# Relu and row sum: the first load of 128 descriptors goes as two loads of 64

## The chip, the cores and the metric

The kernel runs on one core of a Trainium2 chip. The metric is the device time of one execution in microseconds (us), the median of a few runs. Three engines matter here: ScalarE (ACT in the profile) and VectorE (DVE) compute, and SyncE (SP) issues the loads and stores. The data itself is moved by 16 DMA engines that the core shares among all transfers; a profile counts a transfer's time from its issue on SP to its landing, when the last of its pieces has counted up the transfer's semaphore.

## The reference

```python
batch, seq, dim = 32, 512, 1024
x = np.random.randn(batch, seq, dim).astype(np.float32)

def reference(x):
    relu_x = np.maximum(x, 0)
    return np.sum(relu_x, axis=-1).astype(np.float32)
```

So 16,384 rows of 1,024 float32 numbers (67.1 MB) are read, negative numbers become zero, each row is summed, and 16,384 sums (65.5 KB) are written.

## The kernel before

**Regions.** The 16,384 rows are cut along `REGIONS = [1, 111, 16]` (L8) into three parts. In each part every one of the 128 partitions of the on-chip memory holds a stretch of neighbouring rows: 1 row each in the first part, 111 in the second, 16 in the third. Every partition has 128 rows in all. Only the first part is one row deep, so its 128 rows lie next to each other in the input.

**Chunks.** The rows go through three buffers (`buf[:, c % NB, ...]`, L51) of 16 rows per partition, 8 MB each. `CHUNKS` (L9) lists seven full chunks. Chunk 0 is the only one made of two loads: one row of each partition out of the first region, then 15 rows of each out of the second. Each of the six others is one load of 16 rows of each partition. After them come tail loads of 8, 4 and 2 rows, and the last two rows of each partition are cut into four pieces of 912, 512, 256 and 368 numbers (L108 to L115).

**Order of the loads.** All loads are issued by SP in the order in which the loop at L85 writes them, on one queue. From chunk 3 on, each waits until DVE has finished the chunk that used the same buffer (L87). A load over 128 partitions is made of 128 descriptors, one contiguous stretch each: 4 KB in the first load, 60 KB in the second, 64 KB in the chunks after it. The two loads of chunk 0 are moved by hand to the very start of SP's program:

```python
if c == 0:
    code.insert(arrival, code.pop())
    arrival += 1
```

`arrival` is the place ahead of SP's first drain, which belongs to the barrier that all engines pass at the start. So the first two loads are issued before the barrier and everything else behind it.

**Compute.** Both loads of chunk 0 count up the same semaphore `s_in[0]`, by 16 each, and ACT waits for their sum (L140) before it applies relu to the whole chunk in one instruction (L145, 16,384 numbers per partition). DVE then reduces rows in groups (L160). In the later chunks ACT works in pieces, and the last chunk and the tail are split row by row between the two engines, each with an instruction that does relu and sum together (`on_act`, L127; `on_dve`, L130). When the last pieces have landed and been summed, SP stores the sums (L117, L123, L207) and waits for the stores.

Of the kernel before, what the change touches and what calls it, by code (L numbers as in the profile page):

```python
# [3 lines left out]
P = 128  # L4
D = 1024
BIG = 16
NB = 3
REGIONS = [1, 111, 16]  # L8
CHUNKS = [[(0, 0, 1), (1, 0, 15)]] + [[(1, 16 * c + 15, 16)] for c in range(6)]  # L9
ACT_STEPS = [[16], [7, 9], [7, 9], [7, 9], [4, 5, 7], [3, 4, 5]]  # L10
DVE_STEPS = [[4, 5, 7], [7, 4, 5], [7, 4, 5], [7, 4, 5], [4, 5, 7], [3, 4, 5]]
TAIL = [8, 4, 2]
# [4 lines left out]
def bass_relu_sum_kernel(  # L17
# [20 lines left out]
    J = B * S // P  # L38
    NBIG = len(CHUNKS)
    assert BIG * NBIG + sum(TAIL) + 2 == J == sum(REGIONS)  # L40
# [4 lines left out]
    xv = [  # L45
        xr[P * s : P * (s + n), :].rearrange("(p j) d -> p j d", p=P)
        for s, n in zip(start, REGIONS)
    ]
    ov = [of[P * s : P * (s + n)].rearrange("(p j) -> p j", p=P) for s, n in zip(start, REGIONS)]

    buf = nc.alloc_sbuf_tensor("buf", [P, NB, BIG, D], fp32)  # L51
# [6 lines left out]
    s_in = [nc.alloc_semaphore(f"s_in{i}") for i in range(n_in)]  # L58
# [11 lines left out]
    sp, act, dve = nc.sync, nc.scalar, nc.vector  # L70

    NTWO = len(ACT_STEPS)
    done = [sum(map(len, DVE_STEPS[: c + 1])) for c in range(NTWO)]
# [5 lines left out]
    code = nc.main_func.blocks[0].instructions  # L79
    arrival = next(  # L80
        i
        for i, ins in enumerate(code)
        if ins.engine == mybir.EngineType.SP and type(ins).__name__ == "InstDrain"
    )
    for c in range(NBIG + 1):  # L85
        if c >= NB:
            sp.wait_ge(s_dve, done[c - NB])  # L87
        if c < NBIG:
            i = 0
            for g, j, n in CHUNKS[c]:  # L90
                sp.dma_start(  # L91
                    out=buf[:, c % NB, i : i + n, :], in_=xv[g][:, j : j + n, :]
                ).then_inc(s_in[c], 16)
                i += n
                if c == 0:
                    code.insert(arrival, code.pop())
                    arrival += 1
    r = 0
    tail = []
    for i, n in enumerate(TAIL):  # L100
# [10 lines left out]
    for k, (lo, hi) in enumerate((first, second, third)):  # L111
# [6 lines left out]
        out=of[0:P].rearrange("(k q) -> k q", q=32), in_=turned[0:P:32, 0:32]  # L118
# [7 lines left out]
    def on_act(t, acc):  # L126
        return act.activation(t, t, AF.Relu, accum_out=acc)  # L127

    def on_dve(t, acc):
        return dve.tensor_scalar(  # L130
            out=t, in0=t, scalar1=0.0, scalar2=None, op0=ALU.max, op1=ALU.add, accum_out=acc
        )

    def row(c, i):
        return buf[:, c % NB, i, :], res[:, c * BIG + i : c * BIG + i + 1]

    k = 0
    for c in range(NTWO):
        alone = BIG - sum(ACT_STEPS[c])
        act.wait_ge(s_in[c], 16 * len(CHUNKS[c]))  # L140
        r = 0
        ready = []
        for n in ACT_STEPS[c]:
            t = buf[:, c % NB, r : r + n, :]
            act.activation(t, t, AF.Relu).then_inc(s_act, 1)  # L145
            k += 1
            ready += [k] * n
            r += n
        for i in range(BIG - alone // 2, BIG):
            on_act(*row(c, i))  # L150
        if alone:
            dve.wait_ge(s_in[c], 16 * len(CHUNKS[c]))
            for i in range(BIG - alone, BIG - alone // 2):
                on_dve(*row(c, i))
        r = seen = 0
        for n in DVE_STEPS[c]:
            if ready[r + n - 1] > seen:
                seen = ready[r + n - 1]
                dve.wait_ge(s_act, seen)
            dve.tensor_reduce(  # L160
                out=res[:, c * BIG + r : c * BIG + r + n],
                in_=buf[:, c % NB, r : r + n, :],
                axis=X,
                op=ALU.add,
            ).then_inc(s_dve, 1)
            r += n
        if c == 1:
            dve.wait_ge(s_dve, done[c])
            dve.transpose(out=turned[:, :], in_=res[:, 0:32]).then_inc(s_turn, 1)  # L169
# [3 lines left out]
    for c in range(NTWO, NBIG):  # L173
        act.wait_ge(s_in[c], 16 * len(CHUNKS[c]))
        dve.wait_ge(s_in[c], 16 * len(CHUNKS[c]))
        for i in range(BIG):
# [10 lines left out]
    lo, hi = first  # L187
# [5 lines left out]
    lo, hi = second  # L193
    act.wait_ge(s_in[-2], 16)
    on_act(flat[:, lo:hi], seam[:, k + HEAD : k + HEAD + 1]).then_inc(s_seam, 1)
    lo, hi = third
# [41 lines left out]
```

## Time and profile before

| | |
|---|---|
| median of 3 runs | 160.88 us (160.72 to 160.93) |
| span of the profiled execution | 159.4 us |
| DVE busy | 120.6 us (76%) |
| ACT busy | 101.5 us (64%) |
| read from memory | 67.11 MB, 421 GB/s over the span |
| the first load, 512 KB | issued at 0.00 us, landed 3.3 us later |
| the second load, 7,680 KB | issued at 0.45 us, landed 21.1 us later |
| last store | issued at 157.93 us, landed 1.4 us later |

The span runs from the first instruction of the program to the last. The first instruction is the issue of the first load. The profiled execution has no time of its own beside its span, so its time is put together: the span of 159.4 us, and about 1.5 us around it that make up the difference to the median of the runs.

Times in the profile are microseconds from the start of the span. A line such as `SPq L91` is SP issuing a load at line 91. `DMA buf<-in_x_dram` is a load into `buf`. In the list of DMA issues the last number is the time from the issue to the landing, and it includes the time in which a load stands in the queue behind earlier ones.

### The profile page before, as it was taken

What the parts mean: (1) busy time and instruction counts of PE and PEld (TensorE: products, weight loads), DVE (VectorE), ACT (ScalarE), POOL (GpSimd) and SP (SyncE); (2) the same over time, 40 slices, a digit from 0 to 9 for tenths busy, and PEclk for the clock granted to TensorE, in tenths of its full rate; (3) what the DMA queues carried; (4) which work ended last, traced back from release to release, by engine and by line L of the source; (5) the groups of instructions that cost most, each with busy time, mean ns of one, the idle gap of its engine ahead of it and who ended that gap; (6) DMA issues with size and microseconds to landing.
All of it is one profiled execution on the core that took longest, in us unless ns stands there. A gap on an engine that the chain in (4) does not pass through costs nothing.

```text
span 159.4 us, 150 instructions
## 1 busy us (share of the span) xinstructions
DVE 120.6 (76%) x59; ACT 101.5 (64%) x54; POOL 0.2 (0%) x4
## 2 busy tenths in 40 slices
DVE  0000000009999999999999999999999999898995
ACT  3000059980799708996099941999329980496975
POOL 0000000000000000000000000000000000000000
DMA  9997996996996997989979969969969979798994
GB/s 378 493 401 339 493 526 263 526 526 263 526 493 296 526 444 345 526 378 411 526 312 477 526 263 526 526 263 526 526 263 526 444 345 526 321 469 374 417 400 142
DMA packets 2457, 67.18 MB, mean 421 GB/s; under 512 B 536, under 2 KB 792, under 8 KB 1176
## 3 DMA queue, kind: packets, MB, share of 16 engines
q1 hardware_dynamic: 2456, 67.18, 98.1%
q14 instruction: 1, 0.01, 0.0%
HBM read 67.11 MB, written 0.07 MB: 421 GB/s over the span
## 4 chain that ended last, share of the span: by engine, by line
DVE 55%; DMA 34%; ACT 9%; SPq 2%; issue 0%
DVE res L160 54%; DMA buf<-in_x_dram 34%; ACT buf L145 9%; SPq L101 1%; SPq L112 1%; DVE buf L130 0%; DVE seam L130 0%; SPq L91 0%; DVE turned L169 0%
## 5 line engine op out<-in xcount | busy, mean ns | idle before, releaser
L160 DVE TENSOR_REDUCE res<-buf 128x4 f32<-128x4096 f32 (+3 forms) x18 | 99.4, 5596 | 35.5 <-ACT buf L145 35.5
L145 ACT ACTIVATE buf<-buf 128x7168 f32<-128x7168 f32 (+5 forms) x13 | 80.4, 6233 | 46.1 <-DMA buf<-in_x_dram 46.1
L127 ACT ACTIVATE buf<-buf 128x1024 f32<-128x1024 f32 (+2 forms) x19 | 19.0, 999 | 8.9 <-DMA buf<-in_x_dram 8.9
L130 DVE TENSOR_SCALAR_CACHE_REDUCE buf<-buf 128x1024 f32<-128x1024 f32 (+2 forms) x19 | 20.7, 1143 | 1.7 <-DMA buf<-in_x_dram 1.6
L127 ACT ACTIVATION_READ_ACCUMULATOR buf<-buf 128x1 f32 x19 | 3.6, 188 | 0.0
L145 ACT ACT_TABLE_LOAD x1 | 1.3, 1283 | 1.3 <-PEq L223 1.3
L130 DVE DVE_READ_ACCUMULATOR buf<-buf 128x1 f32 x19 | 1.6, 84 | 0.0
L130 DVE TENSOR_SCALAR_CACHE_REDUCE seam<-seam 128x258 f32<-128x258 f32 x1 | 0.4, 421 | 0.0
L127 ACT ACTIVATE seam<-seam 128x114 f32<-128x114 f32 x1 | 0.3, 300 | 0.1
L169 DVE STREAM_TRANSPOSE turned<-res 128x32 f32<-128x32 f32 x1 | 0.2, 211 | 0.0
L127 ACT ACTIVATION_READ_ACCUMULATOR seam<-seam 128x1 f32 x1 | 0.2, 186 | 0.0
L223 POOL MEMSET const-bfloat16-1.0<- 128x1 bf16 x1 | 0.1, 101 | 0.0
L223 POOL MEMSET const-uint8-127<- 128x1 uint8 x1 | 0.1, 101 | 0.0
L223 POOL MEMSET const-float32-0.0<- 128x1 f32 x1 | 0.1, 98 | 0.2 <-issue 0.2
L223 POOL MEMSET const-float32-1.0<- 128x1 f32 x1 | 0.1, 98 | 0.0
L130 DVE DVE_READ_ACCUMULATOR seam<-seam 128x1 f32 x1 | 0.1, 82 | 0.0
## 6 DMA issues: line engine op xcount, KB each, us to landing
buf<-in_x_dram SPq DMA_DIRECT2D x1, 7680.0 KB, 21.1
buf<-in_x_dram SPq DMA_DIRECT2D x1, 4096.0 KB, 25.3
buf<-in_x_dram SPq DMA_DIRECT2D x1, 2048.0 KB, 29.9
buf<-in_x_dram SPq DMA_DIRECT2D x1, 1024.0 KB, 31.9
buf<-in_x_dram SPq DMA_DIRECT2D x1, 512.0 KB, 3.3
buf<-in_x_dram SPq DMA_DIRECT2D x1, 456.0 KB, 32.5
buf<-in_x_dram SPq DMA_DIRECT2D x1, 256.0 KB, 32.7
seam<-in_x_dram SPq DMA_DIRECT2D x1, 184.0 KB, 32.6
```

The lines of the kernel that those rows point to most:

```text
L101: sp.dma_start(out=buf[:, tb, r : r + n, :], in_=xv[-1][:, r : r + n, :]).then_inc(s_in[NBIG + i], 16)
L112: sp.dma_start(out=flat[:, lo:hi], in_=rows[:, lo:hi]).then_inc(s_in[NBIG + len(TAIL) + k], 16)
L127: return act.activation(t, t, AF.Relu, accum_out=acc)
L130: return dve.tensor_scalar(out=t, in0=t, scalar1=0.0, scalar2=None, op0=ALU.max, op1=ALU.add, accum_out=acc)
L145: act.activation(t, t, AF.Relu).then_inc(s_act, 1)
L160: dve.tensor_reduce(out=res[:, c * BIG + r : c * BIG + r + n], in_=buf[:, c % NB, r : r + n, :], axis=X, op=ALU.add,).then_inc(s_dve, 1)
L169: dve.transpose(out=turned[:, :], in_=res[:, 0:32]).then_inc(s_turn, 1)
L223: nc = _bacc.Bacc("TRN2", target_bir_lowering=False, num_devices=1)
```

## The change

A list `STEPS` says into how many loads each entry of `CHUNKS` is cut along the partitions. It is 2 for the first load and 1 for everything else. The first load, 128 partitions by one row, becomes a load of partitions 0 to 63 and a load of partitions 64 to 127, 64 descriptors of 4 KB each, issued one after the other ahead of the 15-row load. All three are moved ahead of SP's drain and count up `s_in[0]`, whose target for ACT becomes 48 in place of 32. The data, their places and all other instructions stay.

```diff
+STEPS = [[2, 1]] + [[1]] * 6
...
             i = 0
-            for g, j, n in CHUNKS[c]:
-                sp.dma_start(
-                    out=buf[:, c % NB, i : i + n, :], in_=xv[g][:, j : j + n, :]
-                ).then_inc(s_in[c], 16)
+            for (g, j, n), step in zip(CHUNKS[c], STEPS[c]):
+                m = P // step
+                for lo in range(0, P, m):
+                    sp.dma_start(
+                        out=buf[lo : lo + m, c % NB, i : i + n, :], in_=xv[g][lo : lo + m, j : j + n, :]
+                    ).then_inc(s_in[c], 16)
+                    if c == 0:
+                        code.insert(arrival, code.pop())
+                        arrival += 1
                 i += n
-                if c == 0:
-                    code.insert(arrival, code.pop())
-                    arrival += 1
...
-        act.wait_ge(s_in[c], 16 * len(CHUNKS[c]))
+        act.wait_ge(s_in[c], 16 * sum(STEPS[c]))
...
-            dve.wait_ge(s_in[c], 16 * len(CHUNKS[c]))
+            dve.wait_ge(s_in[c], 16 * sum(STEPS[c]))
```

## The prediction

> **What bounds the kernel now.** I read the page's busy rows and DMA rows first, then the chain that ended last, then the waits, then windows over the stages, and at last the records of the single packets.
>
> The page, activity in 40 slices and the DMA queue:
>
> ```profile
> span 159.4 us, 150 instructions
> ...
> DVE 120.6 (76%) x59; ACT 101.5 (64%) x54; POOL 0.2 (0%) x4
> ...
> q1 hardware_dynamic: 2456, 67.18, 98.1%
> ```
>
> No compute engine is full, and the queue of loads is: its packets fill 98.1% of what 16 DMA engines have in the span. The chain seems to say something else:
>
> ```profile
> 0.00 0.39 SPq L91
> 0.39 0.05 issue
> 0.45 21.14 DMA buf<-in_x_dram
> ...
> 35.50 34.59 DVE res L160 x6
> ...
> 70.33 51.73 DVE res L160 x9
> 122.05 0.02 issue
> 122.07 0.33 SPq L101
> ...
> 124.39 32.60 DMA buf<-in_x_dram
> ```
>
> It runs through DVE, since SP waits for DVE to free a buffer before it issues the next load. But that wait does not bind. Two lines of the waits and two of the DMA issues show it:
>
> ```profile
> ACT buf L145 <- DMA buf<-in_x_dram: 46.1, 6, 19.1
> ...
> SPq L101 <- DVE res L160: 16.9, 1, 16.9
> ```
>
> ```profile
> buf<-in_x_dram SPq DMA_DIRECT2D x1, 4096.0 KB, 25.3
> ...
> buf<-in_x_dram SPq DMA_DIRECT2D x1, 512.0 KB, 3.3
> ...
> out_dram<-res SPq DMA_DIRECT2D x1, 8.0 KB, 1.4
> ```
>
> The 4,096 KB load, issued at 122.07 when DVE let it go, took 25.3 us to land, though its bytes take 4.19 MB / 434 GB/s = 9.7 us; some 15 us it stood behind the chunk before it. The engines had work queued throughout, and ACT waited for data in every chunk. Windows give the stages (busy time of each engine, then granted clock, DMA share and GB/s):
>
> ```profile
> 0.00:1.00 1.00, 0.00 (x0) 0.00 (x0) 0.20 (x4) 1.00 0.00 0
> 1.00:2.50 1.50, 0.00 (x0) 1.23 (x1) 0.00 (x0) 1.00 1.07 352
> ...
> 40.00:137.00 97.00, 96.97 (x22) 68.60 (x16) 0.00 (x0) 1.00 1.00 434
> ...
> 157.40:159.40 2.00, 0.47 (x4) 0.39 (x2) 0.00 (x0) 1.00 0.16 37
> ```
>
> So this is one stream: nothing moves for 1.0 us, a slower start, 434 GB/s for the body, and 2 us behind the last byte for the last sums and the store. Whatever delays or advances a DMA engine at the start moves the end by as much. A share above 1 means that packets are booked to the window in which they start.
>
> The packet records, joined where one starts as another ends, show the 16 engines. They start the first load one after the other, from 1.012 to 1.357 us (some 20 ns apart). An engine moves 8 packets of 4 KB: the first takes 0.20 to 0.62 us, the others mostly 159 ns (25.8 GB/s, 16 engines 412), but nine of these took 273 to 338 ns. The engines begin the 60 KB packets of the second load between 2.499 and 2.943 us.
>
> **The change part by part.** The profiled execution is span 159.4 plus 1.5 around it, which brings it to the median of the runs, 160.88; I take the 1.5 as unchanged.
>
> *One more issue on SP.* The first issue takes 0.39 us with a gap of 0.05, the second 0.42. The 15-row load is then issued at about 0.90 instead of 0.45. From issue to the engines' first packets took 1.01 to 1.36 us, so its descriptors are there at 1.9 to 2.3 us. The engines reach them between 2.50 and 2.94: 0.6 us of cover, cost 0. Without that cover it would be 0.45. The second half, issued at 0.45, is ready at 1.46 to 1.81; the engines have done 4 packets at 1.012 + 0.62 + 3 x 0.159 = 2.11 (first engine) and about 1.9 (fifth): cover 0.4, cost 0.
>
> *What is queued behind it.* SP's drain, the barrier, and so the load of ACT's table (1.27 to 2.55) come 0.45 later. ACT's first work is at 21.61, 19 us of cover. The load of chunk 1, issued at 1.27, comes at 1.72, and its first packets run at 20.74. POOL's four constants do not move. The later waits of SP for DVE move with the data. ACT waits for 48 in place of 32; the 15-row load still comes last. All at 0; if ACT's cover of 19 us or chunk 1's were gone, 0.45.
>
> *16 more semaphore packets.* One per engine, 9 ns and 6 ns to the next: +0.015.
>
> *An earlier start.* The engines start 20 ns apart with 8 descriptors and a semaphore packet each; with 4 and one, half of the spread of 0.345 might go: 0 to -0.17 for the engine that starts last. If the issue also halves, -0.2 more: together -0.37, the lower end.
>
> *64 partitions at a time.* No load in the trace goes to half of the partitions, so I bound it. Lower end: the engines keep 159 ns per packet, cost 0. Upper end: the limit is not in the engine but in the place where it writes (or reads), and with 16 engines on half of the places each packet of a half takes twice as long: 4 x 159 ns more in each half, 8 x 0.159 = +1.27. What decides is whether two engines that meet at one place slow each other. The nearest rows are the nine packets of 273 to 338 ns: about 2 x 159 = 318, as if two had met. The body's rate says nothing either way, 27.1 GB/s per engine with every load over 128 partitions. I lean to the upper end. Two that share run apart by as much as they started apart: offset d saves 2d, since each runs alone for d in each half. With 8 places in the order between partners, d is about 0.17 and the cost 1.27 - 0.34 = 0.93; with neighbours as partners it stays 1.25.
>
> [...]
>
> Sum for the likeliest: 0.93 + 0.015, less a few hundredths of the earlier start, +0.9 us: span 160.3, time 161.8. Its own range is 161.5 (all of the 0.17 gained, d larger) to 162.2.
>
> **The rivals.**
>
> *Hidden (no change).* The halves run at full rate, since the DMA engine itself is the limit. For it: 159 ns is near the 4,096 B / 27.1 GB/s = 151 ns of the body, so an engine's own pace explains most packets, and the doubled ones can come from the reading side. Then -0.17 to +0.02: 160.7 to 160.9.
>
> *Faster.* The start of the stream binds, and 64 descriptors get it going sooner. Place: the empty first 1.0 us, before which nothing can move. It decides if the halves run at full rate and the issue to first packet shrinks by over 0.32 us; the full price is -0.37: 160.5. Against it: the 8 KB store, with 128 tiny descriptors, still took 1.4 us to land, and 16 starts at 20 ns are the smaller part of the 1.0 us.
>
> *A gap in supply.* The halves run at full rate, but the third issue takes longer than the 0.42 seen, or its descriptors queue behind two others: if the 0.6 us of cover went, up to +0.45: 161.3.
>
> **How the numbers follow.** About 0.2%, 0.32 us, is what a measurement of this kernel can tell from no change. Half rate 0.66, gap 0.04: slower 0.70. Hidden 0.19: same. Faster start 0.11. The time is the likeliest case's, 161.8. The range leaves out the far faster case alone: it goes down past the hidden one to 160.6, and up to 1.27 + 0.015 with a little for the scatter of the runs (0.1), 162.3.
>
> **What would show it.** In the changed profile: three SP issues before 1.4 us in place of two, and two 256 KB loads in place of the 512 KB one. Right, if the 4 KB packets mostly take about 300 ns, the 60 KB packets begin at 3.3 to 3.9 us instead of 2.5 to 2.94, ACT's first relu moves from 21.61 to about 22.5, and every later landing by the same 0.9, with 434 GB/s unchanged in the body. Wrong, if the packets stay at 159 ns (hidden or faster: then the first packet's time against 1.012 tells which), if the engines show an empty stretch between the 4 KB and the 60 KB packets (the gap), or if a shift at the start is made up by the end.

## The result, and the profile after

The changed kernel takes 162.82 us (median of 6 runs), the kernel before 160.90 us (median of 6). The ratio is 1.0114, 95% interval 1.0078 to 1.0151 (without the run of 164.33 us, which counts as slow, being over 1.5% above the fastest): the change costs about 1.9 us, by the interval 1.3 to 2.4. It also makes the time uncertain. The six runs lie between 161.77 and 164.33 us, those of before between 160.72 and 160.97. The profile below is of the run of 161.77 us, so it shows 1.0 us of the loss, not the whole.

The page of the changed kernel, its span, its busy engines and its DMA queue:

```profile
span 160.4 us, 151 instructions
...
DVE 120.6 (75%) x59; ACT 101.6 (63%) x54; POOL 0.2 (0%) x4
...
q1 hardware_dynamic: 2472, 67.18, 97.8%
```

The engines compute as long as before (DVE 120.6 us), one instruction and 16 packets are new, and the same 67.18 MB are moved. The span is longer by 1.0 us. The chain of waits (start, duration, what) says where:

```profile
0.00 0.58 SPq L94
0.58 0.04 issue
0.62 0.59 SPq L94
1.21 0.04 issue
1.25 21.36 DMA buf<-in_x_dram
22.61 0.02 issue
22.64 13.87 ACT buf L148
...
125.37 32.64 DMA buf<-in_x_dram
158.01 0.02 issue
```

Two things are to be seen. The two halves took SP 0.58 and 0.59 us to issue, where the whole load took 0.39, so the 15-row load was issued at 1.25 us instead of 0.45. And ACT's first relu starts at 22.64 instead of 21.61, 1.03 us later; its line in the kernel before is

```profile
21.61 13.87 ACT buf L145
```

The last load of the chain, issued at 125.37, takes as long as before (32.64 us against 32.60): the whole loss is made in the first microseconds and carried to the end.

The DMA issues (KB each, time from issue to landing) and two windows (duration, busy time of the engines, granted clock, DMA share, GB/s):

```profile
buf<-in_x_dram SPq DMA_DIRECT2D x1, 7680.0 KB, 21.4
...
buf<-in_x_dram SPq DMA_DIRECT2D x3, 256.0 KB, 3.8
```

```profile
1.00:2.50 1.50, 0.00 (x0) 0.27 (x1) 0.00 (x0) 1.00 0.72 235
...
40.00:137.00 97.00, 96.97 (x23) 68.60 (x16) 0.00 (x0) 1.00 1.00 432
```

The body runs at 432 GB/s as before (434). The line of three loads of 256 KB holds the two halves and one of the pieces at the end. From 1.0 to 2.5 us 235 GB/s were moved, against 352 before. The packet records fill this in. The first packet runs at 1.363 us instead of 1.012. The 64 packets of the first half take 159 ns in the median, those of the second half 259. The DMA engines begin their 60 KB packets between 3.08 and 4.17 us (before: 2.50 to 2.94). Fifteen have begun by 3.64, and the last only after standing empty for at least 0.5 us. The first 60 KB packets take 2.63 us in the median instead of 2.31. The engine that stood empty stays the last: it reaches the 64 KB packets of chunk 1 at 22.28 us and the next one at 22.10, where the last one of the kernel before is there at 21.27. So some 0.8 us of the 1.0 in this profile would be there without the empty stretch.

So there are three suspects: the half of the partitions, the late 15-row load, and the longer issue itself. The expectations below call them the places theory, the supply theory and the issue theory.

### The profile page after: what moved, and what is told of

Its sections match the earlier page's. It is cut to its first block, busy times and chain, and to the rows that moved or that the text cites. A ratio compares the mean times of both kernels' runs of the same rounds, so it can differ in the third digit from the quotient of the medians.

```text
span 160.4 us, 151 instructions
## 1 busy us (share of the span) xinstructions
DVE 120.6 (75%) x59; ACT 101.6 (63%) x54; POOL 0.2 (0%) x4
## 2 busy tenths in 40 slices
DMA packets 2473, 67.18 MB, mean 419 GB/s; under 512 B 552, under 2 KB 808, under 8 KB 1192
## 3 DMA queue, kind: packets, MB, share of 16 engines
q1 hardware_dynamic: 2472, 67.18, 97.8%
## 4 chain that ended last, share of the span: by engine, by line
DVE 54%; DMA 34%; ACT 9%; SPq 2%; issue 0%
DVE res L163 54%; DMA buf<-in_x_dram 34%; ACT buf L148 9%; SPq L104 1%; SPq L94 1%; SPq L115 1%; DVE buf L133 0%; DVE seam L133 0%; DVE turned L172 0%
## 5 line engine op out<-in xcount | busy, mean ns | idle before, releaser
L133 DVE TENSOR_SCALAR_CACHE_REDUCE buf<-buf 128x1024 f32<-128x1024 f32 (+2 forms) x19 | 20.7, 1143 | 1.7 <-DMA buf<-in_x_dram 1.6
```

What stands on the lines that cost most here:

```text
L133: return dve.tensor_scalar(out=t, in0=t, scalar1=0.0, scalar2=None, op0=ALU.max, op1=ALU.add, accum_out=acc)
```

## The experiments

In what follows "before" is the kernel before on the same chip in the same series; its medians were 160.79, 160.85, 160.81 and 160.83 us in the four series. "Lag" is the time from the issue of the first load to that of the 15-row load.

**The change once more.** No edit.

> The changed kernel once more, for the spread of its runs (161.77 to 164.33 us) and a second profile. Places theory (16 engines that write 64 neighbouring partitions meet in pairs and slow each other by varying amounts): median again 162 to 163.5, a spread of over 1.5 us, and in the profile 4 KB packets of the second half at 250 ns and more, the engines reaching the 60 KB packets at varying times, the last of them at 3.9 us or later. Issue theory (an SP issue of 64 partitions is slow, 0.58 us against 0.39, and pushes everything back): the issues again 0.55 to 0.6 us, the first packet at 1.3 to 1.4, and the time 161.8 to 162.1 with little spread.

Measured: 162.57 us (162.51 to 162.72), ratio 1.0111 (1.0097 to 1.0126). SP's first issues took 0.59, 0.59 and 0.59 us, the first packet ran at 1.37, the packets of the second half took 286 ns in the median, and the last engine began its 60 KB packets at 4.54 us, the others by 3.96. The spread inside this series was only 0.2 us, so the large spread of the first six runs does not come back each time. The signs of the places theory and of the issue theory are there at once; this run does not decide.

**Two halves by columns.** Each load spans all partitions and half of a row.

```diff
-                m = P // step
-                for lo in range(0, P, m):
+                m = D // step
+                for lo in range(0, D, m):
                     sp.dma_start(
-                        out=buf[lo : lo + m, c % NB, i : i + n, :], in_=xv[g][lo : lo + m, j : j + n, :]
+                        out=buf[:, c % NB, i : i + n, lo : lo + m], in_=xv[g][:, j : j + n, lo : lo + m]
```

> The first load goes as two loads of all 128 partitions, 512 numbers each (2 KB descriptors), so there is one issue more, 16 more semaphore packets, and no half of the partitions. Places theory: packets of 2 KB at 80 to 90 ns, the 60 KB packets begin within 0.2 us of where they did before (2.5 to 2.94 plus any delay of the first packet), time 160.7 to 161.2, spread under 0.4. Issue theory: the extra issue alone does it, time 161.6 to 162.3.

Measured: 163.16 us, ratio 1.0148 (1.0134 to 1.0162). This is worse than the change, though no load touches half of the partitions. The issues took 0.39, 0.42 and 0.43 us and the 2 KB packets 84 ns in the median, both as expected. But the 15-row load, issued at 0.91 us, found its engines empty: most had finished the first row by 2.8 us, and they began the 60 KB packets one by one until 5.31 us, the last ones more than 2 us after they had run dry. So a loss of this size comes about without any half. The issue theory is not borne out either: it expected 161.6 to 162.3, and no issue was slow.

**Every other partition.** Two loads of 64 descriptors, the even and then the odd partitions.

```diff
-                m = P // step
-                for lo in range(0, P, m):
+                for lo in range(step):
                     sp.dma_start(
-                        out=buf[lo : lo + m, c % NB, i : i + n, :], in_=xv[g][lo : lo + m, j : j + n, :]
+                        out=buf[lo:P:step, c % NB, i : i + n, :], in_=xv[g][lo:P:step, j : j + n, :]
```

> Two loads of 64 descriptors of 4 KB as in the change, but the first takes the even and the second the odd partitions. Places theory (neighbouring partitions 0 to 63 lie behind half of the places, every other partition behind all): packets back at 159 ns, time 160.7 to 161.2, spread under 0.4. Issue theory, or a cost of 64 descriptors as such: as the changed kernel, 161.7 to 162.8.

Measured: 163.53 us (162.69 to 163.79), ratio 1.0161 (1.0134 to 1.0187). The packets are back at 159 ns in the second half, against 259 and 286 in the two profiles of the change: the slow packets came with 64 neighbouring partitions and not with every other one. But the time did not fall. SP's issues were again slow (0.58, 0.59, 0.59), and two engines stood empty for at least 1.3 us before their first 60 KB packet, which they began at 4.66. What the packets won, the wait for the 15-row load took, and more: in the same series the change itself took 162.57 us.

**Halves of the 15-row load.** The first load whole, the 7.9 MB load in two halves of the partitions.

```diff
-STEPS = [[2, 1]] + [[1]] * 6
+STEPS = [[1, 2]] + [[1]] * 6
```

> The first load stays whole and the 15-row load (7.9 MB) goes as partitions 0 to 63, then 64 to 127. Places theory: 60 KB packets at up to 4.5 us instead of 2.27, 8 of them per engine, so between +8 us (partners run apart) and +18 us: 169 to 179. Issue theory: one issue more behind the start, hidden, 160.8 to 161.3.

Measured: 181.48 us, ratio 1.1271 (1.1246 to 1.1296). The windows of this run, in the stretch in which the halves move:

```profile
2.50:21.00 18.50, 0.00 (x0) 1.07 (x1) 0.00 (x0) 1.00 1.03 218
21.00:40.00 19.00, 0.00 (x0) 0.00 (x0) 0.00 (x0) 1.00 1.00 207
40.00:137.00 97.00, 81.19 (x16) 69.75 (x10) 0.00 (x0) 1.00 1.00 432
```

The engines are full (share 1.03 and 1.00) and move 207 to 218 GB/s, half of the 432 that they reach later in the same run. The median 60 KB packet takes 4.80 us instead of 2.27, 2.1 times as long. This shows the price of a half of neighbouring partitions, 20.7 us on 7.9 MB, a little above the expected range's end. The slowing that the prediction bet on is real; at what "places" the packets meet is not shown.

**A tiny load between.** The kernel before, with 16 descriptors of 64 B between the two loads of chunk 0, into a tile that nothing reads.

```diff
                 if c == 0:
                     code.insert(arrival, code.pop())
                     arrival += 1
+                    if i == 1:
+                        sp.dma_start(out=spare[0:P:8, :], in_=xr[0:P:8, 0:16]).then_inc(s_in[0], 16)
+                        code.insert(arrival, code.pop())
+                        arrival += 1
...
```

(ACT's wait for chunk 0 counts the tiny load too.)

> The kernel before, with a tiny load more between the first load and the 15-row load: 16 descriptors of 64 B, one per engine, into a tile that nothing reads; ACT waits for it too. It adds an issue ahead of the 15-row load and almost no data. Supply theory (the 15-row load, issued third at about 0.9 us, has its descriptors at the engines too late, up to 4.4 us after the issue as in the run by columns): empty stretches before the 60 KB packets on several engines, the last one beginning at 3.5 us or later, time 161.5 to 163.5. Places theory alone: a hidden issue, engines at the 60 KB packets by 3.0 us, time 160.7 to 161.0.

Measured: 162.25 us (162.01 to 162.85), ratio 1.0099 (1.0075 to 1.0123). The tiny load moves 1 KB in all and costs 1.4 us, three quarters of what the change costs. Its issue took 0.61 us, so in these runs a load over less than 128 partitions was slow to issue, with 16 (0.61) as with 64 (0.58 and 0.59), against 0.39 for the first load over 128. The chain of this run:

```profile
0.00 0.39 SPq L92
0.39 0.05 issue
0.44 0.61 SPq L100
1.05 0.04 issue
1.09 21.84 DMA buf<-in_x_dram
```

The 15-row load was issued at 1.09 us, and the engines began it between 2.52 and 4.10 us, five of them at 3.67 us or later, though the last 4 KB packet of all was over at 2.98.

**Three whole loads.** One row, one row, 14 rows, all over 128 partitions.

```diff
-CHUNKS = [[(0, 0, 1), (1, 0, 15)]] + [[(1, 16 * c + 15, 16)] for c in range(6)]
+CHUNKS = [[(0, 0, 1), (1, 0, 1), (1, 1, 14)]] + [[(1, 16 * c + 15, 16)] for c in range(6)]
```

> Chunk 0 as three loads over all 128 partitions: one row (4 KB descriptors), one row, 14 rows (56 KB). The third issue comes at 0.9 us, but the engines have twice the work ahead of it, until about 4.0 us. Supply theory: the third load's descriptors come at 2.8 to 5.3 us, so gaps of up to 1 us on a few engines, time 161.0 to 162.2, less than by columns (163.2). Places theory alone: no gap, 160.7 to 161.1. A theory in which each load that starts by strided rows starts badly: as the kernel before, within 0.3.

Measured: 161.92 us (161.02 to 162.12), ratio 1.0055 (1.0035 to 1.0075). The third load was issued at 0.89 us and had its engines' work until about 4.0 us as cover. Most engines went on to it without a pause, but six stood empty first, for 0.4 us in the mean, and the last began it at 4.60 us. So an engine can take up a load that is issued at 0.9 us as much as 3.7 us later, with nothing else left to do.

**Control: the 15-row load first.**

```diff
-CHUNKS = [[(0, 0, 1), (1, 0, 15)]] + [[(1, 16 * c + 15, 16)] for c in range(6)]
+CHUNKS = [[(1, 0, 15), (0, 0, 1)]] + [[(1, 16 * c + 15, 16)] for c in range(6)]
```

(The rows keep their places in the buffer, by an edit not shown.)

> Control for the next run: the two loads of chunk 0 as before, but the 15-row load is issued first and the one-row load second, whole. Both theories: no engine runs empty, the body as before; the time is that of the kernel before plus or minus what the first packets of 60 KB cost against 4 KB, 160.5 to 162.

Measured: 161.41 us, ratio 1.0038 (1.0023 to 1.0053). No engine runs dry. What is new is the slow first packet of each engine: 60 KB in 3.03 us in the median, against 2.27 for those that follow, and 2.31 for the first ones in the kernel before, where the small load goes ahead. The two engines that began last did so 1.70 and 1.82 us after the issue.

**The halves behind the 15-row load.** As the control, with the one-row load in two halves of neighbouring partitions.

```diff
-STEPS = [[1, 1]] + [[1]] * 6
+STEPS = [[1, 2]] + [[1]] * 6
```

> As the control, with the one-row load behind the 15-row load cut into partitions 0 to 63 and 64 to 127. The engines have 18 us of work ahead of the halves and of what follows, so supply can't matter. Places theory: 4 KB packets at 250 to 320 ns, +0.5 to +1.3 us against the control. Supply theory alone: the same time as the control within 0.2.

Measured: 162.89 us, 1.48 us above the control and a little more than the places theory expected. With 18 us of work ahead (8 packets of 60 KB per engine at 2.27 us) nothing can come late, so this is the price of the halves alone. The packets of the second half take 279 ns in the median (the control's 159). The rest is a surprise: the first 64 KB packets after the halves take 2.70 to 3.22 us instead of 2.42 on all engines.

**More cover.** Whole loads of 1, 3 and 12 rows.

```diff
-CHUNKS = [[(0, 0, 1), (1, 0, 15)]] + [[(1, 16 * c + 15, 16)] for c in range(6)]
+CHUNKS = [[(0, 0, 1), (1, 0, 3), (1, 3, 12)]] + [[(1, 16 * c + 15, 16)] for c in range(6)]
```

> Chunk 0 as whole loads of 1, 3 and 12 rows. There are three issues ahead, as in the run with three whole loads, but 4 KB plus 12 KB packets give the engines work until about 6.3 us. Supply theory (the third load's descriptors come late): they are there in time, no gap before the 48 KB packets, time 160.8 to 161.2. Theory that a third load as such is bad: as with three whole loads, 161.7 to 162.2.

Measured: 160.89 us (10 runs, 160.81 to 160.93), ratio 1.0002 (0.9993 to 1.0012). Three loads, three issues, 16 semaphore packets more, and no cost: the third load, issued at 0.91 us, had until 6 us to arrive. A third load as such was harmless here; what cost in the other runs with a third load was its lateness.

**The 15-row load alone later.** Nothing is cut; only the first load is moved ahead of the barrier.

```diff
-                if c == 0:
+                if c == 0 and g == 0:
                     code.insert(arrival, code.pop())
```

> The kernel before, with the 15-row load left behind the barrier: it is the second load still, but issued at about 1.2 us in place of 0.45, about as late as in the changed kernel (1.25). Supply theory as lateness alone: empty stretches and slow first 60 KB packets as in the changed kernel, 161.7 to 163. Theory that a third load is what is slow (the descriptors of the loads ahead are made first): the second load's descriptors come 1.0 to 1.4 us after the issue, at 2.2 to 2.6 us, in time: 160.7 to 161.1.

Measured: 162.67 us (161.25 to 163.39), ratio 1.0103 (1.0048 to 1.0158). This is the whole loss of the change, and its scatter, without any half and without any load more. The 15-row load was issued at 0.80 us instead of 0.45. Chain and DMA issues of this run:

```profile
0.80 23.51 DMA buf<-in_x_dram
24.32 0.02 issue
24.34 13.87 ACT buf L145
```

```profile
buf<-in_x_dram SPq DMA_DIRECT2D x1, 7680.0 KB, 23.5
...
buf<-in_x_dram SPq DMA_DIRECT2D x1, 512.0 KB, 3.5
```

The profiled run is the longest of the four (163.39 us). Issued 0.36 us later, the load lands 23.5 us after its issue instead of 21.1, so 2.7 us later in all. By the packet records, 12 engines begin it between 2.65 and 3.10 us, four at 4.14, 5.13, 5.25 and 5.58 us, up to 4.8 us after the issue, though all 4 KB packets were over at 3.10. One page line, ACT's busy share in 40 slices, shows what the reader would see first, in the kernel before and in this run:

```profile
ACT  3000059980799708996099941999329980496975
...
ACT  3000009994299924999069970899519990397976
```

ACT's first relu has moved a slice to the right, and the work after it has moved with it.

**The tiny load behind.** As with the tiny load between, but issued after the 15-row load.

```diff
-                    if i == 1:
+                    if i == BIG:
```

> The tiny load of 16 descriptors, issued behind the 15-row load in place of ahead of it. Supply theory: nothing is late, 160.8 to 161.1, against 162.25 with the same tiny load ahead. If the tiny load itself costs time: 161.5 or more.

Measured: 160.85 us (10 runs, 160.74 to 160.90), ratio 1.0002 (0.9993 to 1.0011), against 162.25 with the same load ahead. Its chain shows the 15-row load in the place that it has in the kernel before:

```profile
0.00 0.38 SPq L92
0.38 0.05 issue
0.44 0.43 SPq L92
0.86 0.04 issue
0.91 20.87 DMA spare<-in_x_dram
```

The tiny load's slow issue (0.60 us), its 16 semaphore packets and the later barrier cost nothing that can be measured.

**Two queues.** The halves on SP, the 15-row load issued by ACT ahead of its drain.

```diff
-                    sp.dma_start(
+                    (act if c == 0 and g else sp).dma_start(
...
```

> The two halves on SP as in the change, the 15-row load issued by ACT ahead of its drain, at about 0.1 us, so it stands behind no other issue. Supply theory: no engine runs empty before its 60 KB packets, whatever the halves cost, and the time falls to 160.6 to 161.6. Places theory alone: as the changed kernel, 161.8 or more, since the halves still meet at half of the places.

Measured: 164.40 us, ratio 1.0212 (1.0191 to 1.0233), worse than the change. The engines did get the 15-row load early (first packets 1.15 to 2.08 us), but then took packets of the two queues in turn: the first 4 KB packet ran at 3.97 us, and the last at 24.6, so ACT's first work had to wait for them. The 60 KB packets took about 2.65 us for the whole of that time. By its time it falls where the places theory alone put it (161.8 or more), but the run was meant to cure the lateness and brought a trouble of its own, so it counts for neither theory.

**Both loads later.** Neither is moved ahead of the barrier, so they start later, one right after the other.

```diff
-                if c == 0:
-                    code.insert(arrival, code.pop())
-                    arrival += 1
```

> The kernel before with both loads of chunk 0 left behind the barrier, one right after the other. The 15-row load comes as late in absolute time as in the run with that load alone behind the barrier (issue at 0.8 us or later: 162.67), but only 0.45 us after the first load. Lag theory (what counts is how long after the first load it is issued, since the engines already run at full rate when its descriptors come): no empty stretch, first 60 KB packets below 2.5 us, and only the shift of the start itself, 0.3 to 0.8: 161.0 to 161.7. Absolute theory (any load issued after 0.6 us is slow to reach the engines): 162.5 to 164.

Measured: 161.52 us (161.46 to 161.59), ratio 1.0045 (1.0027 to 1.0063).

```profile
0.73 0.39 SPq L91
1.12 0.06 issue
1.19 21.11 DMA buf<-in_x_dram
```

The 15-row load is issued at 1.19 us, nearly as late as in the changed kernel (1.25), but 0.46 us after the first load, and it lands after 21.1 us as in the kernel before. The loss is the later start: first packet at 1.743 instead of 1.012, 0.73 us, against 0.7 measured. So it is the lag that counts.

**Engines idle.** A tiny load ahead, the 15-row load behind the barrier, the one-row load after it.

```diff
-CHUNKS = [[(0, 0, 1), (1, 0, 15)]] + [[(1, 16 * c + 15, 16)] for c in range(6)]
+CHUNKS = [[(1, 0, 15), (0, 0, 1)]] + [[(1, 16 * c + 15, 16)] for c in range(6)]
...
+    sp.dma_start(out=spare[0:P:8, :], in_=xr[0:P:8, 0:16]).then_inc(s_in[0], 16)
+    code.insert(arrival, code.pop())
     for c in range(NBIG + 1):
...
-                if c == 0:
-                    code.insert(arrival, code.pop())
-                    arrival += 1
```

> A tiny load of 16 descriptors goes ahead, and the 15-row load is issued behind the barrier at about 0.8 us, with the one-row load behind it. The engines are idle when its descriptors come. Busy theory (descriptors reach engines late when these run at full rate): the first 60 KB packets of all 16 engines begin 1.0 to 1.5 us after the issue, within 0.6 us of each other (two stragglers to 0.8 as in the run with the 15-row load first), 161.8 to 162.4, which is that run's 161.41 plus the later start. Late-issue theory: they spread over 2 us and more, up to 4 us after the issue, 163 or more.

Measured: 162.71 us (162.69 to 162.72), ratio 1.0118 (1.0102 to 1.0134), above the expected range. The issue came at 1.27 us, not 0.8, as the tiny load's own issue took 0.63. Set against that, the picture is the expected one: 13 engines begin 0.97 to 1.26 us after the issue, three at 1.48, 1.49 and 1.73. The first packet is 1.23 us later than in the control with the 15-row load first, and 161.41 + 1.23 = 162.64. Into idle engines the 15-row load got within 2.0 us of its issue in the four runs where it met them (the longest, 1.97 us, with two queues), into running ones it took up to 4.8.

**A lag of 0.6.** The 15-row load behind SP's drain but ahead of its wait at the barrier.

```diff
                 if c == 0:
                     code.insert(arrival, code.pop())
-                    arrival += 1
+                    arrival += 2
```

> The kernel before with the 15-row load behind SP's drain but ahead of its barrier wait: issued some 0.6 us after the first load, between the 0.45 of before (160.8) and the 0.8 of the run with that load behind the barrier (162.67). A cover that runs out steadily as the lag grows: 161.2 to 162.2 with a few engines empty for under 1 us. A sharp edge above 0.6: 160.8 to 161.1. A sharp edge below 0.6: 162.3 to 163.

Measured: 160.91 us in the median of 10 runs, but from 160.76 to 163.16, ratio 1.0027 (0.9996 to 1.0057). Six runs are those of the kernel before (160.76 to 160.93), four lie at 161.18, 161.42, 161.43 and 163.16. At a lag of 0.64 us the load mostly still comes in time, and sometimes does not. It is an edge, and this kernel stands close to it.

**All together.** The issue of the 15-row load, which is also its lag where the first load is issued at 0.00, the time at which the last engine began its 60 KB packets (in the one profile of each run), and the time:

| run | issue of the 15-row load, us | last engine begins it, us | median (range), us |
|---|---|---|---|
| before | 0.45 | 2.94 | 160.90 (160.72 to 160.97) |
| tiny load behind | 0.44 | 3.04 | 160.85 (160.74 to 160.90) |
| lag 0.6 | 0.64 | 2.95 | 160.91 (160.76 to 163.16) |
| 15-row load later | 0.80 | 5.58 | 162.67 (161.25 to 163.39) |
| by columns | 0.91 | 5.31 | 163.16 (163.07 to 163.33) |
| tiny load between | 1.09 | 4.10 | 162.25 (162.01 to 162.85) |
| the change | 1.25 | 4.17 | 162.82 (161.77 to 164.33) |
| the change once more | 1.26 | 4.54 | 162.57 (162.51 to 162.72) |
| every other partition | 1.25 | 4.66 | 163.53 (162.69 to 163.79) |
| both later | 1.19, lag 0.46 | 3.56 | 161.52 (161.46 to 161.59) |

Up to a lag of 0.46 us nothing is lost by it, at 0.64 us in most executions nothing. Above it the loss jumps to 1.4 to 2.7 us and hardly grows with the lag. This shows that a 15-row load issued too long after the first is by itself enough for the whole loss, and that a third load which is not late costs nothing. It does not show how the 1.9 us of the change divide. The halves by themselves cost 1.48 us where nothing is late, and in the two profiles of the change only one engine stood empty for long (0.5 us or more) before its 60 KB packets. The two causes do not add up there: with every other partition the packets were fast and the time was no lower. A run with the halves in front and more work ahead of the 15-row load would tell what is left once the lateness is gone; there is none. Why running engines take up a new load so late is not shown. The packet records tell when an engine begins, not whether it had its descriptors by then. No variant was faster than the kernel before.

## Why the prediction was wrong

It forecast slower, 161.8 us with a range to 162.3; the time is 162.82, outside. The direction was right, and the halves do slow packets (259 ns in the second half of the change, against 159). But a term that the sum put at nothing is enough for the whole loss by itself.

- **What bounds the kernel.** Right. The stream of loads is the bound, the body kept its rate (432 GB/s against 434), and the shift of the start (ACT's first relu 1.03 us later) is the shift of the end (span 1.0 us longer). The 1.5 us around the span were 1.4 (161.77 less 160.4).
- **One more issue on SP.** This is the step that failed. It put the third issue at 0.90 us, its descriptors at the engines 1.01 to 1.36 us later, and so found 0.6 us of cover. Both halves of that are wrong. The issues of loads over 64 partitions took 0.58 us, and the one after them 0.59, so the third came at 1.25. And the 1.01 to 1.36 us was read from the first load, which meets idle engines. The runs show 0.97 to 1.97 us into idle engines, but up to 4.8 us into running ones (15-row load later). The price given for the cover being gone, 0.45, was one issue's length; what the runs with a late 15-row load lost, from a lag of about 0.6 us on, was 1.4 to 2.7.
- **What is queued behind it** (barrier, table load, chunk 1). Right: with the tiny load behind, all of these came later and the time was 160.85.
- **16 semaphore packets.** Right: the same run and the one with more cover have them, at 1.0002 of the kernel before each.
- **An earlier start.** Wrong in sign. With 64 descriptors the issue took 0.19 us more, and the first packet ran 0.35 us later (1.363 against 1.012), where the prediction had it no later.
- **64 partitions at a time.** Right that the packets slow down: twice the time per packet in the large halves (4.80 us against 2.27), 259 ns in the second half of the change. That engines meet in pairs at half of the places was an assumption and the 0.17 us between partners an estimate from the spread of the starts (0.345 us); no run shows either. The term's size was 0.93; the halves cost 1.48 us where they stand behind other work. Wrong that both halves are slowed alike: the first was hardly slowed at all (159 ns in the median). What the term adds in the change itself is not shown. With every other partition the packets took 159 ns and the time was not lower, so the slow packets seem to pass while the engines would otherwise wait for the 15-row load.
- **The rivals.** "A gap in supply" named the wait that counts, a third issue over 0.42 us and a cover that goes, though with halves at full rate; it had a chance of 0.04 and a price of up to 0.45 us. The +0.9 of the sum came close to the one profiled run (161.77), and so did two of its signs (ACT's first relu at 22.64, forecast 22.5; fifteen engines at the 60 KB packets by 3.64, forecast 3.3 to 3.9). That is in good part luck. The loss of that run is made up of a first packet 0.35 us later, a second half at 259 ns, first 60 KB packets of 2.63 us instead of 2.31, and one engine that stood empty; the sum had the slow packets alone.

## What to carry to other kernels

The time from a load's issue to its first packet, read off where the DMA engines are idle, is not the time that it takes while they run: here 1.0 to 2.0 us became up to 4.8. So a load that must follow another without a gap was safe here in two ways only: issued right behind it, at a lag of 0.45 us, or with several microseconds of work ahead of it (work until 4.0 us was too little for a load issued at 0.9, work until about 6 was enough). A load of 1 KB in between cost 1.4 us. Where a prediction costs a moved issue at nothing, the cover should be several times the latency that was read (here up to 4.8 us came in place of 1.01 to 1.36), and a run with that one issue delayed settles it.

## What the runs showed of the hardware that was not expected

- A load over fewer than 128 partitions held SP for 0.55 to 0.63 us (16 or 64 partitions; 0.82 once), one over 128 at the same place for 0.38 to 0.43. In the changed kernel and with the tiny load between, the issue after it was slow as well (0.59 and 0.57 us), though it goes over 128 partitions.
- The first large packets after a start from idle or after halves were slow together: 3.03 us in the median for 60 KB (15-row load first), 2.70 to 3.22 us for 64 KB behind the halves, against 2.27 and 2.42 for those that follow. It lasts for one packet per engine in these two runs; where the engines began far apart (by columns), the second packet of those that began early was slow too, 2.91 to 3.15 us. Why is open.
- Two queues with large and small packets at once took turns packet by packet: the 4 KB packets of the halves were spread from 3.97 to 24.6 us between packets of 60 KB (two queues).
